# Weights on 128 partitions, and a first image load split over two queues, in a 3x3 convolution

## The chip, the cores and the metric

The kernel runs on one core of a Trainium2 chip. The metric is the time of one execution on the device in microseconds, the median of several. The core has a matrix engine (TensorE, PE in the profile, with PEld for its weight loads), a vector engine (VectorE, DVE), a scalar engine (ScalarE, ACT), a general one (GpSimd, POOL) and SyncE (SP), which in this kernel only issues DMAs. The 16 DMA engines are shared by all queues: SP's queue is q1 in the profile, ScalarE's is q10. Matmuls write PSUM; everything else lies in SBUF.

## The reference

A 3x3 convolution with padding 1 over 16 images of 64 channels and 64x64 pixels, float32, with 64 output channels, and a residual of the output's shape added:

```
x: (16, 64, 64, 64)   weight: (64, 64, 3, 3)   residual: (16, 64, 64, 64)
output[b, co] += weight[co, ci, kh, kw] * x_pad[b, ci, kh:kh+h, kw:kw+w]   # for all b, co, ci, kh, kw
return output + residual
```

The images, the residual and the output are 16.8 MB each.

## The kernel before, in words

**Data.** Two images make a pair: 128 partitions (image and channel) by 4096 pixels, one DMA of 2 MB with a row of 16 KB for each partition. There are 8 pairs. Three buffers `xr` hold pairs of images as they come; eight buffers `ro`, one for each pair, hold the residual, to which the result is added in place, and which is then stored. ScalarE casts each image to bf16 into one of four buffers `xp`, even rows of pixels into partitions 64 to 127 (line 159) and odd rows into partitions 0 to 63 (line 163), so that one matmul with 128 rows works on two rows of pixels at once.

**Weights.** ScalarE's queue loads them (line 151) as 64 partitions (output channel) by 576 numbers (input channel and tap). TensorE transposes the nine taps with an identity matrix that GpSimd makes (line 195), into PSUM buffer 0. VectorE casts six blocks of 64x192 from there into `wl` (line 172), in the layout of the stationary operand: d is which of two neighbouring rows, kw the column of the tap, and par says whether the output row is even or odd. GpSimd zeroes the two blocks that no tap fills (lines 147 and 148). The last cast raises `s_bank` by 2, which lets TensorE use both PSUM buffers.

**The convolution.** For each image, TensorE runs six steps (kw, d) of four matmuls each: four chunks of 8 row pairs by 64 columns, a whole PSUM buffer in all (line 83 issues a matmul with its weight load, line 84 one without). That makes 24 matmuls an image, 384 in all. Two PSUM buffers take turns. It waits for `s_bank` (the buffer is free) and `s_pack` (the image is cast) before each image. VectorE adds the residual in two instructions for each image (line 182) and raises `s_add`.

**Order of the work.** All waits are written out by hand.
- SP's program: pair 0 of the images (line 71), put by `to_the_front` ahead of everything else in its program, then residual 0, images 1, residual 1 and so on. From the fourth pair on, an image load waits on `s_half` until ScalarE has done with the buffer. The stores of pairs 0 to 4 (line 77) follow, each behind a wait on `s_add`. The stores of pairs 5 to 7 come after the critical section, which ends when all engines are done with it.
- ScalarE's program: the weights' DMA, then for each image its two casts; the first image of a pair waits for the landing of that pair (`s_x`).
- TensorE's program: a wait for the identity and the zeroed parts (`s_id`), a wait for the weights (`s_w`), the nine transposes, then a loop over four rounds of four images.
- GpSimd's program: the identity, the zeroes of the padding rows, the zeroes in `wl`.

Of the kernel before, what the change touches and what calls it, by code (L numbers as in the profile page):

```python
# [8 lines left out]
FP32 = mybir.dt.float32  # L9
# [6 lines left out]
def kernel(  # L16
# [7 lines left out]
    nc = tc.nc  # L24
# [6 lines left out]
    NPIX = H * W  # L31
# [4 lines left out]
    NXR = 3  # L36
# [3 lines left out]
    res_bc = residual.rearrange("b c h w -> (b c) (h w)")  # L40
    out_bc = out.rearrange("b c h w -> (b c) (h w)")
    x_bc = x.rearrange("b c h w -> (b c) (h w)")
    w_flat = weight.rearrange("co ci kh kw -> co (ci kh kw)")

    pool = ctx.enter_context(tc.tile_pool(name="pool", bufs=1))
    psum = ctx.enter_context(tc.tile_pool(name="psum", bufs=1, space=bass.MemoryType.PSUM))

    ident = pool.tile([64, 64], FP32)
    ro = [pool.tile([128, NPIX], FP32, name=f"ro{p}") for p in range(NPAIR)]
    xr = [nc.alloc_sbuf_tensor(f"xr{i}", [128, NPIX], FP32) for i in range(NXR)]  # L50

    xp = [pool.tile([128, J + 1, W], BF16, name=f"xp{i}") for i in range(NXP)]
    wraw = nc.alloc_sbuf_tensor("wraw", [64, 576], FP32)
    wl = pool.tile([128, 2, 3, 2, 64], BF16)
    ps = [psum.tile([128, NCHUNK, JC, W], FP32, name=f"ps{i}") for i in range(2)]

    sem = lambda name: tc.alloc_semaphore(name)
    s_w = sem("s_w")
    s_x = [sem(f"s_x{i}") for i in range(NXR)]
    s_r = [sem(f"s_r{p}") for p in range(NPAIR)]  # L60
    s_out = sem("s_out")
    s_id = sem("s_id")
    s_wt = sem("s_wt")
    s_half = sem("s_half")
    s_pack = sem("s_pack")
    s_bank = sem("s_bank")
    s_conv = sem("s_conv")
    s_add = sem("s_add")

    def load_x(p):  # L70
        return nc.sync.dma_start(out=xr[p % NXR][:, :], in_=x_bc[128 * p : 128 * p + 128, :]).then_inc(s_x[p % NXR], 16)

    def load_ro(p):
        nc.sync.dma_start(out=ro[p][:, :], in_=res_bc[128 * p : 128 * p + 128, :]).then_inc(s_r[p], 16)

    def store(p):
        return nc.sync.dma_start(out=out_bc[128 * p : 128 * p + 128, :], in_=ro[p][:, :])

    def matmul(out_, lhsT, rhs, start, stop, ldweights):

        e = nc.tensor
        if ldweights:
            return e.matmul(out=out_, lhsT=lhsT, rhs=rhs, start=start, stop=stop, skip_group_check=True)  # L83
        return e.add_instruction(  # L84
            mybir.InstMatmult(
                name=nc.get_next_instruction_name(),
                engine=PE,
                ins=[e.lower_ap(rhs), e.lower_ap(lhsT)],
                outs=[e.lower_ap(out_)],
                start_tensor_calc=start,  # L90
                stop_tensor_calc=stop,
                tile_size=(128, 128),
                tile_position=(0, 0),
                bass_skip_group_check=True,
                ldweights=False,
            )
        )

    def to_the_front(dma):

        def fixed(ap):
            t = ap.bass_ap.tensor.name
            return mybir.PhysicalAccessPattern(
                ap=ap.ap, offset=ap.bass_ap.offset, dtype=ap.dtype, memref=t, memsetref=t + "_set", bass_ap=ap.bass_ap
            )

        front = nc.main_func.blocks[0].instructions
        here = nc.cur_bb.bb.instructions  # L110
        ins = here.pop()
        assert ins.name == dma.ins.name
        at = next(
            i for i, e in enumerate(front) if e.engine == mybir.EngineType.SP and isinstance(e, mybir.InstDrain)
        )
        front.insert(at, copy.replace(ins, ins=[fixed(a) for a in ins.ins], outs=[fixed(a) for a in ins.outs]))

    with tc.tile_critical(no_gpsimd_drain=True):  # L118

        for p in range(NPAIR):  # L120
            if p >= NXR:

                nc.sync.wait_ge(s_half, 2 * (p - NXR) + 3)
            i = load_x(p)
            if p == 0:
                to_the_front(i)
            load_ro(p)
        for p in range(NEARLY):
            nc.sync.wait_ge(s_add, 2 * p + 3)
            store(p).then_inc(s_out, 16)  # L130


        nc.gpsimd.memset(ident[:, :], 0.0).then_inc(s_id, 1)  # L133
        nc.gpsimd.wait_ge(s_id, 1)
        nc.gpsimd.affine_select(  # L135
            out=ident[:, :],
            in_=ident[:, :],
            compare_op=mybir.AluOpType.not_equal,
            fill=1.0,
            base=0,  # L140
            pattern=[[-1, 64]],
            channel_multiplier=1,
        ).then_inc(s_id, 1)
        for t in xp:
            nc.gpsimd.memset(t[0:64, 0, :], 0.0).then_inc(s_id, 1)  # L145
            nc.gpsimd.memset(t[64:128, J, :], 0.0).then_inc(s_id, 1)  # L146
        nc.gpsimd.memset(wl[0:64, 0, :, 1, :], 0.0).then_inc(s_id, 1)  # L147
        nc.gpsimd.memset(wl[64:128, 1, :, 0, :], 0.0).then_inc(s_id, 1)  # L148


        nc.scalar.dma_start(out=wraw[:, :], in_=w_flat[:, :]).then_inc(s_w, 16)
        for n in range(B):
            p, im = divmod(n, 2)
            hp = slice(64 * im, 64 * im + 64)
            x4 = xr[p % NXR].rearrange("q (j two w) -> q j two w", two=2, w=W)
            t = xp[n % NXP]
            if im == 0:
                nc.scalar.wait_ge(s_x[p % NXR], 16 * (p // NXR + 1))
            i = nc.scalar.copy(out=t[64:128, 0:J, :], in_=x4[hp, :, 0, :])  # L159
            i.then_inc(s_half, 1)  # L160
            if n >= NXP:
                i._wait_ge(s_conv, n - NXP + 1)
            nc.scalar.copy(out=t[0:64, 1 : J + 1, :], in_=x4[hp, :, 1, :]).then_inc(s_pack, 1)  # L163


        nc.vector.wait_ge(s_wt, 1)
        tpf = ps[0].rearrange("p c j w -> p (c j) w")

        blocks = ((0, 0, 0, 0), (1, 0, 0, 1), (1, 0, 1, 0), (0, 1, 0, 2), (0, 1, 1, 1), (1, 1, 1, 2))
        for half, d, par, kh in blocks:  # L170
            hp = slice(64 * half, 64 * half + 64)
            i = nc.vector.tensor_copy(out=wl[hp, d, :, par, :], in_=tpf[0:64, 3 * kh : 3 * kh + 3, :])  # L172
        i.then_inc(s_bank, 2)
        for n in range(B):
            p, im = divmod(n, 2)
            hp = slice(64 * im, 64 * im + 64)
            o4 = ro[p].rearrange("q (j two w) -> q j two w", two=2, w=W)
            psj = ps[n % 2].rearrange("q c j w -> q (c j) w")
            if im == 0:
                nc.vector.wait_ge(s_r[p], 16)  # L180
            for par in range(2):
                i = nc.vector.tensor_tensor(  # L182
                    out=o4[hp, :, par, :], in0=psj[64 * par : 64 * par + 64, :, :], in1=o4[hp, :, par, :], op=ADD
                )
                if par == 0:
                    i._wait_ge(s_conv, n + 1)

                i.then_inc(s_add if par == 0 or n == B - 1 else s_bank, 1)


        nc.tensor.wait_ge(s_id, 4 + 2 * NXP)
        nc.tensor.wait_ge(s_w, 16)
        wraw3 = wraw.rearrange("p (ci t) -> p ci t", t=9)
        for t in range(9):
            i = nc.tensor.transpose(out=ps[0][0:64, t // 8, t % 8, :], in_=wraw3[:, :, t], identity=ident[:, :])  # L195
        i.then_inc(s_wt, 1)
        with nc.Fori(0, B // NXP, 1, engines=[PE]):
            for n in range(NXP):
                nc.tensor.wait_ge(s_bank, 1).then_inc(s_bank, -1)
                nc.tensor.wait_ge(s_pack, 1).then_inc(s_pack, -1)  # L200
                order = [(1, 0), (1, 1), (0, 0), (0, 1), (2, 0), (2, 1)]
                for i, (kw, d) in enumerate(order):
                    xlo, xhi = max(0, 1 - kw), min(W, W + 1 - kw)
                    for c in range(NCHUNK):
                        j0 = JC * c
                        m = matmul(
                            ps[n % 2][:, c, :, xlo:xhi],
                            wl[:, d, kw, :, :].rearrange("q r c -> q (r c)"),
                            xp[n][:, j0 + d : j0 + d + JC, xlo + kw - 1 : xhi + kw - 1],
                            i == 0,  # L210
                            i == len(order) - 1,
                            c == 0,
                        )
                m.then_inc(s_conv, 1)
# [36 lines left out]
```

## Time and profile before

| | |
|---|---|
| median of 3 runs | 124.08 us (124.05 to 124.40) |
| the profiled execution's own time | 124.16 us |
| its span in the profile | 122.1 us |
| TensorE busy | 86.5 us, 71% |
| VectorE busy | 75.2 us, 62% |
| ScalarE busy | 62.0 us, 51% |
| GpSimd busy | 2.2 us |
| moved by DMA | 50.48 MB, mean 413 GB/s over the span |
| from issue to landing, median: images, residual, stores, weights | 17.6, 22.1, 28.7, 8.5 us |

The page of the profile gives the busy time of each engine, its busy share in 40 equal slices of the span (one digit each, in tenths), the DMA queues with packets, megabytes and the share of 16 engines' span, groups of instructions with their mean time and what ended the idle time before them, and the DMA issues. A row of a timeline is the start, the time from the first start to the last end of a run of like instructions, the engine, the line, what it writes from what, the number of instructions, and in brackets how long the engine was idle before and what released it. An engine's name with a q (SPq) is its sequencer, which issues DMAs. The 2.06 us between the span and the time of the profiled execution lie around the traced program.

### The profile page before, as it was taken

The page shows a single profiled execution, that of the slowest core. Times are in us where ns is not written, and L with a number is a line of the kernel's source. Part 1 is how long each engine was busy: PE and PEld are TensorE (multiplying, and loading weights), DVE is VectorE, ACT ScalarE, POOL GpSimd, SP SyncE. Part 2 cuts the span into 40 slices and gives each one's busy share as a digit, 9 for nine tenths or more (in the row PEclk, how much of TensorE's full clock was granted, in tenths as well). Part 3 has the DMA queues.
Part 4 walks back from the last instruction along what each step waited for, and adds up shares of the span by engine and source line. Part 5 has one row for each costly group of instructions (what it writes and reads, how often), then busy time and mean ns, then how long its engine had stood idle before and what let it go on. Part 6 is the DMA issues. An engine that isn't in the chain of part 4 may idle for free.

```text
span 122.1 us, 729 instructions
## 1 busy us (share of the span) xinstructions
PE 86.5 (71%) x389; PEld 10.4 (9%) x105; DVE 75.2 (62%) x38; ACT 62.0 (51%) x33; POOL 2.2 (2%) x16
## 2 busy tenths in 40 slices
PE   0003799999999999999999999999999930000000
PEld 0003000101111010101010101111110100000000
DVE  0004101989889898898989889898798988000000
ACT  4009948966984993992994896699000000000000
POOL 5100000000000000000000000000000000000000
PEclk9999999999999999999999999999999999555555
DMA  6999999999999999999999999999999999999993
GB/s 182 408 348 429 429 429 429 429 424 429 429 429 424 429 429 429 429 429 429 429 429 419 429 429 424 429 429 429 435 435 435 429 429 429 435 435 429 429 429 140
DMA packets 3536, 50.48 MB, mean 413 GB/s; under 512 B 400, under 2 KB 400, under 8 KB 464
## 3 DMA queue, kind: packets, MB, share of 16 engines
q1 hardware_dynamic: 3456, 50.33, 97.8%
q10 hardware_dynamic: 80, 0.15, 0.4%
HBM read 33.70 MB, written 16.78 MB: 413 GB/s over the span
## 4 chain that ended last, share of the span: by engine, by line
PE 70%; DVEq 2%; DVE 2%; issue 0%
PE ps L84 53%; PE ps L83 17%; DVEq L118 2%; DVE ro L182 2%
## 5 line engine op out<-in xcount | busy, mean ns | idle before, releaser
L182 DVE TENSOR_TENSOR ro<-ps,ro 64x2048 f32<-64x2048 f32 x32 | 73.2, 2289 | 17.4 <-PE ps L84 16.9
L84 PE MATMUL ps<-xp,wl 128*128 128x504 bf16 (+1 forms) x288 | 79.9, 387 | 0.2
L159 ACT CAST xp<-xr 64x2048 bf16<-64x2048 f32 x16 | 30.3, 1896 | 21.3 <-DMA xr<-in_x_dram 21.1
L83 PE MATMUL ps<-xp,wl 128*128 128x504 bf16 (+1 forms) x92 | 35.6, 387 | 2.4 <-PEq L200 2.4
L163 ACT CAST xp<-xr 64x2048 bf16<-64x2048 f32 x16 | 30.4, 1897 | 0.4
L83 PEld LDWEIGHTS ps<-xp,wl 128*128 128x128 bf16 x96 | 9.5, 99 | 77.5 <-issue 77.5
L172 DVE CAST wl<-ps 64x192 bf16<-64x192 f32 x6 | 1.9, 347 | 10.9 <-PE ps L195 10.8
L195 PE MATMUL ps<-ident,wraw 64*64 64x64 f32 x9 | 1.1, 305 | 9.6 <-DMA wraw<-in_weight_dram 9.6
L159 ACT ACT_TABLE_LOAD x1 | 1.3, 1283 | 1.5 <-SPq L118 1.5
L195 PEld LDWEIGHTS ps<-ident,wraw 64*64 64x64 f32 x9 | 0.9, 163 | 9.6 <-issue 9.6
L146 POOL MEMSET xp<- 64x64 bf16 x4 | 0.6, 147 | 0.2
L145 POOL MEMSET xp<- 64x64 bf16 x4 | 0.6, 145 | 0.2
L148 POOL MEMSET wl<- 64x192 bf16 x1 | 0.3, 253 | 0.1
L147 POOL MEMSET wl<- 64x192 bf16 x1 | 0.3, 252 | 0.1
L135 POOL TENSOR_SCALAR_AFFINE_SELECT ident<-ident 64x64 f32<-64x64 f32 x1 | 0.2, 233 | 0.2 <-POOL ident L133 0.2
L133 POOL MEMSET ident<- 64x64 f32 x1 | 0.1, 145 | 0.5 <-SPq L118 0.5
L235 POOL MEMSET const-bfloat16-1.0<- 128x1 bf16 x1 | 0.1, 113 | 0.0
L235 POOL MEMSET const-uint8-127<- 128x1 uint8 x1 | 0.1, 112 | 0.0
L235 POOL MEMSET const-float32-1.0<- 128x1 f32 x1 | 0.1, 109 | 0.0
L235 POOL MEMSET const-float32-0.0<- 128x1 f32 x1 | 0.1, 104 | 0.2 <-issue 0.2
## 6 DMA issues: line engine op xcount, KB each, us to landing
xr<-in_x_dram SPq DMA_DIRECT2D x8, 2048.0 KB, 17.6
ro<-in_residual_dram SPq DMA_DIRECT2D x8, 2048.0 KB, 22.1
out_dram<-ro SPq DMA_DIRECT2D x8, 2048.0 KB, 28.7
wraw<-in_weight_dram ACTq DMA_DIRECT2D x1, 144.0 KB, 8.5
```

Of the source, the lines that this page charges most:

```text
L83: return e.matmul(out=out_, lhsT=lhsT, rhs=rhs, start=start, stop=stop, skip_group_check=True)
L84: return e.add_instruction(mybir.InstMatmult(name=nc.get_next_instruction_name(), engine=PE, ins=[e.lower_ap(rhs), e.lower_ap(lhsT)], outs ...
L118: with tc.tile_critical(no_gpsimd_drain=True):
L145: nc.gpsimd.memset(t[0:64, 0, :], 0.0).then_inc(s_id, 1)
L146: nc.gpsimd.memset(t[64:128, J, :], 0.0).then_inc(s_id, 1)
L147: nc.gpsimd.memset(wl[0:64, 0, :, 1, :], 0.0).then_inc(s_id, 1)
L159: i = nc.scalar.copy(out=t[64:128, 0:J, :], in_=x4[hp, :, 0, :])
L163: nc.scalar.copy(out=t[0:64, 1 : J + 1, :], in_=x4[hp, :, 1, :]).then_inc(s_pack, 1)
L172: i = nc.vector.tensor_copy(out=wl[hp, d, :, par, :], in_=tpf[0:64, 3 * kh : 3 * kh + 3, :])
L182: i = nc.vector.tensor_tensor(out=o4[hp, :, par, :], in0=psj[64 * par : 64 * par + 64, :, :], in1=o4[hp, :, par, :], op=ADD)
L195: i = nc.tensor.transpose(out=ps[0][0:64, t // 8, t % 8, :], in_=wraw3[:, :, t], identity=ident[:, :])
L235: nc = _bacc.Bacc("TRN2", target_bir_lowering=False, num_devices=1)
```

## The change

- The weights are loaded as 128 partitions of 288 numbers: half a row (32 input channels) of each output channel on each partition.
- The identity is 128x128. Each of the nine transposes takes 128 partitions by 32 channels and writes 32 partitions by 128 columns of PSUM.
- A block of `wl` is now filled by two casts of 32x192, one for each half of the input channels, which read PSUM with a step of two columns. There are 12 casts: VectorE does those of four blocks, ScalarE those of the other two, after the casts of image 0. Both raise `s_wt`, and TensorE waits for 3 on it (one for its own transposes, one for each of the two engines) before the loop. `s_bank` is raised at VectorE's first cast.
- The first image load is split by columns: pixels 0 to 2047 of pair 0 go by SP's queue, pixels 2048 to 4095 by ScalarE's queue, each at the front of its engine's program; the weights' DMA follows the second half in ScalarE's queue. Waits on `s_x` of buffer 0 count one DMA more.
- GpSimd waits for the identity before it goes on to the zeroes.

```diff
-    w_flat = weight.rearrange("co ci kh kw -> co (ci kh kw)")
+    w_rows = weight.rearrange("co (h ci) kh kw -> (co h) (ci kh kw)", h=2)
...
-    ident = pool.tile([64, 64], FP32)
+    ident = pool.tile([128, 128], FP32)
...
-    wraw = nc.alloc_sbuf_tensor("wraw", [64, 576], FP32)
+    wraw = nc.alloc_sbuf_tensor("wraw", [128, 288], FP32)
...
-    def load_x(p):
-        return nc.sync.dma_start(out=xr[p % NXR][:, :], in_=x_bc[128 * p : 128 * p + 128, :]).then_inc(s_x[p % NXR], 16)
+    def load_x(p, engine=nc.sync, cols=slice(0, NPIX)):
+        return engine.dma_start(out=xr[p % NXR][:, cols], in_=x_bc[128 * p : 128 * p + 128, cols]).then_inc(
+            s_x[p % NXR], 16
+        )
...
         at = next(
-            i for i, e in enumerate(front) if e.engine == mybir.EngineType.SP and isinstance(e, mybir.InstDrain)
+            i for i, e in enumerate(front) if e.engine == ins.engine and isinstance(e, mybir.InstDrain)
         )
...
+    blocks = ((0, 0, 0, 0), (1, 0, 0, 1), (1, 0, 1, 0), (0, 1, 1, 1), (0, 1, 0, 2), (1, 1, 1, 2))
+    tp = ps[0].rearrange("p c j w -> p c (j w)")
+
+    def weight_block(h, half, d, par, kh):
+
+        at = 64 * half + 32 * h
+        return dict(out=wl[at : at + 32, d, :, par, :], in_=tp[0:32, kh, 0:384].rearrange("p (kw co h) -> p kw co h", kw=3, h=2)[:, :, :, h])
...
-            i = load_x(p)
             if p == 0:
-                to_the_front(i)
+                to_the_front(load_x(p, cols=slice(0, NPIX // 2)))
+            else:
+                load_x(p)
             load_ro(p)
...
-            pattern=[[-1, 64]],
+            pattern=[[-1, 128]],
             channel_multiplier=1,
         ).then_inc(s_id, 1)
+        nc.gpsimd.wait_ge(s_id, 2)
...
-        nc.scalar.dma_start(out=wraw[:, :], in_=w_flat[:, :]).then_inc(s_w, 16)
+        to_the_front(load_x(0, nc.scalar, slice(NPIX // 2, NPIX)))
+        nc.scalar.dma_start(out=wraw[:, :], in_=w_rows[:, :]).then_inc(s_w, 16)
...
-                nc.scalar.wait_ge(s_x[p % NXR], 16 * (p // NXR + 1))
+                nc.scalar.wait_ge(s_x[p % NXR], 16 * (p // NXR + 1 + (p % NXR == 0)))
...
+            if n == 0:
+                nc.scalar.wait_ge(s_wt, 1)
+                for b in blocks[4:]:
+                    for h in range(2):
+                        i = nc.scalar.copy(**weight_block(h, *b))
+                i.then_inc(s_wt, 1)
...
         nc.vector.wait_ge(s_wt, 1)
-        tpf = ps[0].rearrange("p c j w -> p (c j) w")
-
-        blocks = ((0, 0, 0, 0), (1, 0, 0, 1), (1, 0, 1, 0), (0, 1, 0, 2), (0, 1, 1, 1), (1, 1, 1, 2))
-        for half, d, par, kh in blocks:
-            hp = slice(64 * half, 64 * half + 64)
-            i = nc.vector.tensor_copy(out=wl[hp, d, :, par, :], in_=tpf[0:64, 3 * kh : 3 * kh + 3, :])
-        i.then_inc(s_bank, 2)
+        for k, b in enumerate(blocks[:4]):
+            for h in range(2):
+                i = nc.vector.tensor_copy(**weight_block(h, *b))
+                if k == h == 0:
+                    i.then_inc(s_bank, 2)
+        i.then_inc(s_wt, 1)
...
         for t in range(9):
-            i = nc.tensor.transpose(out=ps[0][0:64, t // 8, t % 8, :], in_=wraw3[:, :, t], identity=ident[:, :])
+            i = nc.tensor.transpose(
+                out=tp[0:32, t // 3, 128 * (t % 3) : 128 * (t % 3) + 128], in_=wraw3[:, :, t], identity=ident[:, :]
+            )
         i.then_inc(s_wt, 1)
+        nc.tensor.wait_ge(s_wt, 3)
```

## The prediction

> **What bounds the kernel now.** I read the page's slices first, then its DMA queues.
>
> ```profile
> PE   0003799999999999999999999999999930000000
> ...
> DMA  6999999999999999999999999999999999999993
> ...
> q1 hardware_dynamic: 3456, 50.33, 97.8%
> q10 hardware_dynamic: 80, 0.15, 0.4%
> ```
>
> The 16 DMA engines are full from about 1 us until 120.8 us. SP's queue q1 alone takes 97.8% of them: 3072 packets of 16 KB, 192 an engine, at 0.611 us each in the packet records, are 117.3 us. That is the bound. But TensorE's work is almost as long, and it ends where the last stores are waiting for it. The timeline of the start, cut to the rows that carry the first convolution:
>
> ```profile
> 8.89 1.90 ACT L159 CAST xp<-xr 64x2048 bf16<-64x2048 f32 x1 [6.09 <-DMA xr<-in_x_dram]
> ...
> 9.63 1.14 PE L195 MATMUL ps<-ident,wraw 64*64 64x64 f32 x9 [9.63 <-DMA wraw<-in_weight_dram]
> 10.81 1.97 DVE L172 CAST wl<-ps 64x192 bf16<-64x192 f32 x6 [10.81 <-PE ps L195]
> 10.81 1.90 ACT L163 CAST xp<-xr 64x2048 bf16<-64x2048 f32 x1
> ...
> 13.12 0.58 PE L83 MATMUL ps<-xp,wl 128*128 128x512 bf16 x1 [2.35 <-PEq L200]
> ```
>
> Two arms meet at 13.1 us. Image: landing 8.87, two ScalarE casts, 12.71. Weights: landing 9.50, transposes, VectorE casts, 12.78. From there TensorE has no gap until 98.78 us (the groups of instructions have 2.4 us of idle time before line 83, all of it here, and 0.2 before line 84). And the timeline of the end:
>
> ```profile
> 98.78 4.61 DVE L182 TENSOR_TENSOR ro<-ps,ro 64x2048 f32<-64x2048 f32 x2 [0.58 <-PE ps L84]
> 103.68 1.76 SPq L77 DMA_DIRECT2D out_dram<-ro  x3
> ```
>
> The last three stores stand behind the end of the critical section, so they are issued at 103.68, after VectorE's last sum. The engines are then still writing the fifth store, whose landings spread from 105.64 to 106.57. So TensorE has little room: how little decides this case. At the start of the program an issue takes 1.01 (first engine) to 1.43 us (last one) to its first packet; for a store issued into an empty queue I take the same. With empty engines the end follows the issue by 1.43, a restart of 0 to 0.8 us (the 16 first packets of the run averaged 1.31 us for 0.61, the next ones 0.71; I take 0.3), and 24 packets, 14.75 us: 16.5 us. Before, the last packet ended 17.07 us after that issue (103.68 to 120.75). The room is thus 0.6 us (0.1 to 0.9), and every microsecond past it by which the convolution starts later is a microsecond at the end.
>
> **What the Trainium skill says.** "DMA: Bandwidth & Descriptors", section "Queues, rings and completion order": each DMA engine goes round between the queues that have work, a packet at a time. The trace agrees, with one addition. The DMA queues of two stretches, 0 to 5.2 us and 5.2 to 6.2 us:
>
> ```profile
> q1 hardware_dynamic: 86, 1.41, 79.0%
> ```
>
> ```profile
> q1 hardware_dynamic: 25, 0.41, 104.8%
> q10 hardware_dynamic: 25, 0.06, 14.6%
> ```
>
> 25 packets against 25: one 16 KB packet of q1 for each 2.3 KB packet of weights. The addition: the weights' DMA was issued at 0.95, and none of its packets ran before 5.2 us; on the engines that I followed by chaining starts to ends, five or six packets of q1 go first, the one under way and about four more that were already committed. The same page, "Issuing engines are not separate DMA queues": issuing from two engines saves only issue time; all runs on the same 16 DMA engines. So the split image moves no faster. "TensorE: Matmul & The Clock Gate", "Wait — 56ns, not 53.3ns?": from cold, start to start is N / 1.2 GHz. Here the first 128x512 matmuls start 0.427 apart, and the transposes with N=64 fp32 0.107. "VectorE: DVE Perf Modes", "Two Vector instructions with no wait between them": an instruction whose output starts in another quadrant of partitions is held until the one ahead is done. The six casts agree: starts 0.35 to 0.36 apart where the half changes, 0.27 where it stays.
>
> **The change part by part.** *Image split.* Same 2 MB on the same engines: 8 packets of 16 KB an engine become 8 of 8 KB on q1 and 8 on q10. Eight more packets cost below 0.1 us an engine; two queues may shorten the start, which lost 0.8 us an engine, so -0.5 to +0.2. It lies inside the DMA bound; I take 0. SP has as many issues as before, so none is late there; ACT's issue (its weights issue took 0.53) stands ahead of its drain (at 0.13 before) and may hold the opening barrier by 0.1 to 0.2 us, under the image's first 5 us of data.
>
> *Weights on 128 partitions.* Not 4 packets of 2.3 KB an engine but 8 of 1.15 KB; and in q10 they now stand behind the image's second half. While they go, q1 holds the first residual, in 16 KB packets. By the alternation, eight weight packets and the completion let some eight 16 KB packets go by, where four did. Estimate of the landing: 16 KB units x 0.615 + 2.0 (starts at 1.2, the ramp 0.8) + 1.5 or so from mean completion to the last engine's landing. The estimate gives 9.4 for before (9.5 units: eight of image, 0.6 of weights, one of residual; 5.9 + 3.5), measured 9.50. After, with:
> - both halves in step: 4 + 4 units of image, 8 of residual, 0.56 of weights: 16.6 units, 10.2 + 3.5 = 13.7
> - SP's half five packets ahead: q10 finishes four 16 KB packets later, 20.6 units, 12.6 + 3.5 = 16.1
> - ACT's half ahead by as much: 12.6 units, 7.7 + 3.5 = 11.2
>
> SP's first issue stands at 0.00, ACT's first instruction at 0.13, and ACT's issue takes longer; so SP's half is ahead, by three packets I say, between the first two: landing 15.0. That is 5.5 us later.
>
> *Transposes.* Still nine, but with 128 moving columns for 64. At N=64 they start 0.107 apart, so I take 0.213 (0.107 if loads of weights set the pitch): 8 x 0.213 + 0.41 = 2.1 for 1.14 us, +1.0 (0 to 1.0).
>
> *Casts.* The row has 347 ns for 64x192. Twelve half-blocks replace six; VectorE has eight of 32x192, each with another start quadrant than its neighbour: 7 x 0.357 + 0.35 = 2.85 for 1.97 us, +0.9. ScalarE's four: a 2048-wide cast takes 1.90, so 192 columns take some 0.35 by the same fixed part (the Trainium skill, "VectorE: DVE Perf Modes", "The TRN2 errata", prices a ScalarE copy out of PSUM at 172 cycles and one an element at 1.2 GHz, 0.30 us), 1.4 in all, beside VectorE's 2.85, hence nothing. ScalarE is free for them: image 0 lands by 11, its casts end by 15, and the transposes by 17.3. *The wait on s_wt for 3* comes ahead of the loop: 0 to 0.25, I take 0.1.
>
> What is queued behind these waits: on ScalarE, image 1's casts and then image 2's, whose first releases SP's fourth image load. Before, that load went at 20.63 while SP's queue held work until 33.4 (the landing of the third residual); at five to seven microseconds later it is still early, and so are the loads after it.
>
> *Larger identity, moved wait on POOL.* Its fills ended at 3.7 us; twice the columns add tenths. The weights land much later, which hides it; without that, tenths.
>
> *Sum.* Convolution from the weights' landing: 0.13 + 2.1 + 0.04 + 2.85 + 0.31 + 0.1 = 5.55 us, before 3.6. It starts at 15.0 + 5.55 = 20.5 for 13.1: 7.4 later. Less the 0.6 of room: +6.8 with these terms. The transposes and the start's cold stretch (12 matmuls at 0.427, it may be a few more or fewer at 0.21 each) can each give half a microsecond back, so I say +6.4. On the profiled execution: span 122.1 + 6.4 = 128.5 and the same 2.1 us around it, 130.6; the median of the runs, 124.08, stands 0.08 below the profiled execution's 124.16, so 130.5.
>
> **The rivals.** *ACT's half goes first.* Landing 11.2, convolution 16.75, 3.65 late: +3.05, 127.1. For it: nothing orders the two queues. Against it: SP's instruction starts first.
> *All of SP's half is committed ahead* (look-ahead counted in bytes, so eight packets of 8 KB): q10 starts behind it and alternates with 16 KB packets all along: about 24 units, landing 18.5, 11 late, some 134. For it: the four committed packets of before are 64 KB.
> *Not slower: weights pass by.* If the engines serve the short q10 packets together rather than one by one between residual packets, the weights land right behind the image. What decides is their landing: the longer chain costs 1.95 of itself, the room is 0.6, so only a landing before 8.2 us keeps the old end. Then the DMA bound stays, with up to 0.5 gained at the start: 123.5 to 124.4. For it: the queue that sets the bound isn't made longer. Against it: the 25 to 25 above; and the image's own data take until nearly 7.
> *The change doesn't do what it says*: the halves use the same engines, so nothing is doubled; that is in my sum already.
>
> **How the numbers follow.** SP's half ahead by none to five packets: 0.70, from 129 to 132.5, 130.5. ACT's ahead: 0.15. All of SP's half ahead, or a worse restart: 0.08. Not slower: 0.07, of it 0.03 for a gain of over 0.3%, which is about what this measurement can tell from no change. Slower 0.93, same 0.04, faster 0.03. Range 126.6 to 132.8: the first two cases nearly whole.
>
> **What would show it.** Right: weight packets of q10 between residual packets, landing at 13 to 16; transposes 0.21 apart, eight casts in 2.8; the first convolution at 19 to 22; a hole in the DMA slices near 106 to 112 us, ahead of the last three stores; the three issued at about 111. Wrong: the transposes start before 9.5, or the DMA row stays full to the end with a later convolution, which would mean that the room was larger than 0.6.

## The result, and the profile after

The changed kernel takes 129.01 us (median of six runs, 128.58 to 129.98) where the kernel before takes 124.18: a ratio of 1.0395, with a 95% interval of 1.0352 to 1.0437. It is slower, and by a little less than the 130.5 that was forecast. The profiled execution took 128.65 us, with a span of 126.8 for 122.1: +4.7 us.

The page of the kernel after, in the parts that answer to those shown of before:

```profile
PE   0000517999999999999999999999999990000000
...
DMA  6999999999999999999999999999999990199993
...
q1 hardware_dynamic: 3456, 49.28, 91.6%
q10 hardware_dynamic: 288, 1.20, 2.3%
```

The DMA row has a hole in slices 34 and 35 of the 40, where before it was full to the last slice. The convolution starts two slices later (the 5 ahead of it in TensorE's row is the transposes). The start, cut to the rows of the first convolution:

```profile
8.93 1.90 ACT L173 CAST xp<-xr 64x2048 bf16<-64x2048 f32 x1 [6.17 <-DMA xr<-in_x_dram]
10.85 1.90 ACT L177 CAST xp<-xr 64x2048 bf16<-64x2048 f32 x1
...
14.25 2.08 PE L214 MATMUL ps<-ident,wraw 128*32 128x128 f32 x9 [14.25 <-DMA wraw<-in_weight_dram]
16.37 1.27 ACT L182 CAST wl<-ps 32x192 bf16<-32x192 f32 x4 [3.62 <-PE ps L214]
16.45 2.89 DVE L189 CAST wl<-ps 32x192 bf16<-32x192 f32 x8 [16.45 <-PE ps L214]
...
19.77 0.58 PE L85 MATMUL ps<-xp,wl 128*128 128x512 bf16 x1 [3.44 <-PEq L222]
```

The image's arm is where it was: its casts run from 8.93 to 12.75, before from 8.89 to 12.71. Only the weights are late: they land at 14.12 us (before 9.50), and the chain behind them takes 5.65 us for 3.6. The convolution starts at 19.77, 6.64 us later. And the end:

```profile
104.91 4.61 DVE L201 TENSOR_TENSOR ro<-ps,ro 64x2048 f32<-64x2048 f32 x2 [0.58 <-PE ps L86]
109.81 1.78 SPq L79 DMA_DIRECT2D out_dram<-ro  x3
```

The last three stores are issued 6.13 us later than before. How DMA went meanwhile, from the table of stretches of the kernel after (start and end, length, busy time and instructions of PE, PEld, DVE, ACT and POOL, the granted clock of TensorE, the DMA engines' busy share, GB/s):

```profile
105.00:110.00 5.00, 0.00 (x0) 0.00 (x0) 4.49 (x2) 0.00 (x0) 0.00 (x0) 0.91 0.00 0
110.00:111.00 1.00, 0.00 (x0) 0.00 (x0) 0.00 (x0) 0.00 (x0) 0.00 (x0) 0.50 0.61 262
```

In five microseconds only VectorE works, and no byte moves. By the packet records the hole reaches from 105.40 to 110.64.

### The profile page after: what moved, and what is told of

It reads as the page before. It is cut to its first block, busy times and chain, and to the rows that moved or that the text cites. A ratio compares the mean times of both kernels' runs of the same rounds, so it can differ in the third digit from the quotient of the medians.

```text
span 126.8 us, 741 instructions
## 1 busy us (share of the span) xinstructions
PE 87.2 (69%) x393; PEld 10.7 (8%) x105; DVE 76.0 (60%) x40; ACT 63.2 (50%) x37; POOL 2.4 (2%) x16
## 4 chain that ended last, share of the span: by engine, by line
PE 67%; DVEq 2%; DVE 2%; issue 0%
PE ps L86 50%; PE ps L85 17%; DVEq L129 2%; DVE ro L201 2%
## 5 line engine op out<-in xcount | busy, mean ns | idle before, releaser
L189 DVE CAST wl<-ps 32x192 bf16<-32x192 f32 x8 | 2.8, 348 | 16.6 <-PE ps L214 16.4
L214 PE MATMUL ps<-ident,wraw 128*32 128x128 f32 x9 | 2.1, 416 | 14.3 <-DMA wraw<-in_weight_dram 14.3
L182 ACT CAST wl<-ps 32x192 bf16<-32x192 f32 x4 | 1.2, 308 | 3.7 <-PE ps L214 3.6
L214 PEld LDWEIGHTS ps<-ident,wraw 128*32 128x32 f32 x9 | 1.2, 141 | 14.7 <-issue 14.2
```

The costliest lines, as they stand in the source:

```text
L182: i = nc.scalar.copy(**weight_block(h, *b))
L189: i = nc.vector.tensor_copy(**weight_block(h, *b))
L214: i = nc.tensor.transpose(out=tp[0:32, t // 3, 128 * (t % 3) : 128 * (t % 3) + 128], in_=wraw3[:, :, t], identity=ident[:, :])
```

## The experiments

All comparisons are with runs of the kernel before on the same chip, whose medians were 124.15 to 124.21. "Landing" is that of the weights, "start" the first matmul of the convolution.

| kernel | landing | start | last three stores issued | median us | ratio to before, 95% interval |
|---|---|---|---|---|---|
| before | 9.50 | 13.13 | 103.68 | 124.18 | |
| changed | 14.12 | 19.77 | 109.81 | 129.01 | 1.0395 (1.0352 to 1.0437) |
| split only | 12.83 | 16.47 | 107.24 | 125.91 | 1.0122 (1.0095 to 1.0150) |
| 128 partitions only | 10.85 | 16.51 | 107.34 | 125.69 | 1.0101 (1.0051 to 1.0150) |

**Each half of the change alone.** First the image split without the new weights:

```diff
 # before, with the changed kernel's load_x, to_the_front and count on s_x
-                to_the_front(i)
+                to_the_front(load_x(p, cols=slice(0, NPIX // 2)))
...
+        to_the_front(load_x(0, nc.scalar, slice(NPIX // 2, NPIX)))
         nc.scalar.dma_start(out=wraw[:, :], in_=w_flat[:, :]).then_inc(s_w, 16)
```

> The kernel before with only the image split: pixels 0 to 2047 by SP's queue, 2048 to 4095 by ScalarE's queue, both at the front; the weights stay on 64 partitions (4 packets of 2.3 KB an engine) and follow the image half in ScalarE's queue. Theory (each weight packet waits for one packet of the other queue): four packets fewer than in the changed kernel, 4 x 0.62 us, so the weights land at 11.6 instead of 14.1; the chain behind them is the old 3.6 us, the convolution starts at 15.2; by the rule that the span is the convolution's start plus 107.3 (changed kernel: 126.8 - 19.8 + 0.3 for its shorter cold stretch), 122.5, some 124.5 us in all. Rival (the cut into 128 partitions makes the delay, the place in the queue does not): the weights land near 9.5 as before, 123.3 to 124.1 us.

Then the new weights with the old image load:

```diff
 # the changed kernel
-                to_the_front(load_x(p, cols=slice(0, NPIX // 2)))
+                to_the_front(i)
...
-        to_the_front(load_x(0, nc.scalar, slice(NPIX // 2, NPIX)))
         nc.scalar.dma_start(out=wraw[:, :], in_=w_rows[:, :]).then_inc(s_w, 16)
```

> The changed kernel with the image load of before: the whole first pair by SP's queue, nothing of it in ScalarE's. The weights on 128 partitions, the 128-wide transposes and the twelve casts stay. Theory: eight weight packets wait for eight of SP's where four did, so they land at 9.5 + 4 x 0.62 = 12.0; 5.6 us of chain, the convolution starts at 17.6, span 124.9, some 126.9 us. Rival (the image half ahead of the weights makes the whole delay): landing near 9.5, convolution at 15.1, 124.4 us.

Neither rival holds, and both landings were missed, in opposite directions: 12.83 for the expected 11.6, 10.85 for the expected 12.0. So were the times, 125.91 for 124.5 and 125.69 for 126.9. The sums had one price for both kinds of weights, and the packet records show two. From the first weights packet to the last it took 3.05 us in before and 3.14 with the split only, where each engine has four of them, and 4.89 us in both kernels with eight: 1.8 us more, where four packets at 0.62 would make 2.5. The last landing then followed the last packet by 1.17 to 1.24 us with 64 partitions and by 0.94 with 128. The part on the stream's lead, below, has the slower packets behind the first of these. The delays of the convolution add up all the same: 3.34 us for the split, where the landing makes all of it, and 3.38 for the 128 partitions, where the landing makes 1.35 and the longer chain 2.0. The sum is 6.72, and the whole change has 6.64. The times do not add up: +1.7 and +1.5 against +4.8, because the end hides 1.6 to 1.9 us of either delay, by the medians, and hides it once.

**Do the two queues take turns by packets, or by bytes?** In the kernel after, the DMA queues from 8.3 to 13.2 us, while the weights' packets run (queue: packets, MB, share of 16 engines):

```profile
q1 hardware_dynamic: 132, 1.90, 90.6%
q10 hardware_dynamic: 132, 0.15, 8.3%
```

132 against 132, although the one kind has 16 KB and the other 1.15. The test makes SP's packets smaller and leaves their bytes:

```diff
     def load_ro(p):
-        nc.sync.dma_start(out=ro[p][:, :], in_=res_bc[128 * p : 128 * p + 128, :]).then_inc(s_r[p], 16)
+        parts = 4 if p == 0 else 1
+        for c in range(parts):
+            cols = slice(c * NPIX // parts, (c + 1) * NPIX // parts)
+            nc.sync.dma_start(out=ro[p][:, cols], in_=res_bc[128 * p : 128 * p + 128, cols]).then_inc(s_r[p], 16)
...
-                nc.vector.wait_ge(s_r[p], 16)
+                nc.vector.wait_ge(s_r[p], 64 if p == 0 else 16)
```

> The changed kernel with the first residual loaded in four DMAs of a quarter of its columns, so packets of 4 KB instead of 16 KB; same bytes, same order in SP's queue. Theory (one packet against one, whatever their size): some 13 packets of ScalarE's queue (image and weights) wait 0.15 instead of 0.61 us each, the weights land about 5.5 us earlier, near 8.6; the convolution starts near 14.2, and the end is set by DMA again, 123.3 to 123.8 us. Rival (the queues share by bytes or by time): the weights land near 14 as in the changed kernel, 128.6 to 129.4 us.

The weights land at 10.01, 4.1 us earlier than in the changed kernel, and the time falls to 124.68 (ratio to before 1.0039, 1.0020 to 1.0058). From 7.2 to 9.5 us, while the weights run:

```profile
q1 hardware_dynamic: 158, 0.58, 76.2%
q10 hardware_dynamic: 153, 0.16, 21.1%
```

Again one packet against one. Sharing by bytes or by time is ruled out. The gain is short of the expected 5.5 us, and the end is therefore not quite set by DMA: a hole of 1.5 us is left ahead of the last stores. The 4 KB packets took 0.20 us each in this stretch, not the 0.15 that was assumed, and with 0.06 for a packet of weights a turn took 0.25 us. That is part of the miss; the rest is open.

**How much room has the end?** Twelve more casts on VectorE delay the convolution and touch no DMA:

```diff
 # before
+    spare = nc.alloc_sbuf_tensor("spare", [128, 12, 192], BF16)
...
+        for b, (half, d, par, kh) in enumerate(2 * blocks):
+            nc.vector.tensor_copy(out=spare[64 * half : 64 * half + 64, b, :], in_=tpf[0:64, 3 * kh : 3 * kh + 3, :].rearrange("p a b -> p (a b)"))
         for half, d, par, kh in blocks:
```

> The kernel before with twelve more casts of the same kind on VectorE ahead of the six that fill wl, into a spare tile that nobody reads; all loads are unchanged. The convolution starts 12 x 0.328 = 3.9 us later, at 17.1. Theory with the room that the changed kernel's trace shows (start plus 107.3): span 124.4, some 126.4 us. The prediction's room of 0.6 us: 124.1 + 3.9 - 0.6 = 127.4 us. Rival (the start of the convolution is covered by DMA): 124.1 us.

The start moves by 3.81 us to 16.93, and the median is 126.52 (ratio 1.0175, 1.0135 to 1.0215): 2.3 us for 3.8. A late start alone, with the loads as they were, costs time at the end. For the size of the room the test decides less. The median lies by the 126.4 of the larger room, and the four runs, 126.00 to 126.98, stay below the 127.4 of the smaller. But in the profiled execution, which took 126.84, the last stores are issued 3.43 us later than before and the span is 2.93 longer: a room of 0.5. From that issue to the last packet it took 16.53 us here, and 15.63 to 15.74 in the changed kernel and in the three others above; the first packets of the 16 engines start over 0.61 us, in those four over 0.15. Why is open.

**Is the hole all?** The next edit leaves the late start and takes away what makes the last stores wait for VectorE's very last sum:

```diff
 # the changed kernel
-    NEARLY = 5
+    NEARLY = 8
```

> The changed kernel with all eight stores inside the critical section (NEARLY 8 instead of 5), each behind its own wait on s_add, so that the stores of pairs 5 and 6 no longer stand behind VectorE's very last sum. Nothing at the start is changed. Theory (the time is lost only in the hole ahead of the last three stores): the hole closes or nearly so, only the last store needs the last sum, near 109.6, and then it has 4.9 us to go; DMA sets the end, and its stream is 0.9 us ahead of before's: span 121.3 to 122, 123.3 to 124 us, although the convolution starts as late as in the changed kernel. Rival (something else in the late start costs time): it stays near 128 to 129 us.

123.24 us, 0.9925 of before (0.9910 to 0.9940). The convolution starts at 19.51, VectorE ends at 109.44, as late as in the changed kernel, and the hole is gone. The page and the stretch that held the hole:

```profile
DMA  6999999999999999999999999999999999999992
```

```profile
104.00:110.00 6.00, 0.80 (x4) 0.00 (x0) 4.83 (x3) 0.00 (x0) 0.00 (x0) 0.93 0.99 423
```

So the whole loss lies in the hole. The control gives the edit to the kernel before:

```diff
 # before
-    NEARLY = 5
+    NEARLY = 8
```

> The kernel before with all eight stores inside the critical section, and nothing else: the control for the changed kernel with that edit. Theory (before is bound by its DMA stream, and has 1.4 us of room at the end): no change, 124.0 to 124.3 us. Rival (the place of the last stores costs time of itself): 123.3 us, as the changed kernel with this edit.

124.55, which is 1.0026 of before (1.0013 to 1.0040): no gain, rather a loss of 0.3 us, which neither the theory nor the rival had. The traces show where most of it lies: from the last packet to the end of the span it is 1.66 us, before 1.34, and all three versions with early stores have 1.66 or 1.67. So this edit makes the program's end 0.3 us longer. The early stores are no gain of themselves; they remove what the late start costs.

**Where does the stream's lead come from?** With the stores early, the changed kernel is 0.9 us faster than before. Not all of this is the stream: the span of the profiled execution is 0.65 us shorter, and the rest lies outside the span. The time of a run exceeds its span by 2.06 to 2.10 us, on average, in before and in three of the variants, and by 1.76 to 1.82 in all with the new weights. The version with the twelve casts, which has the old weights, also has 1.81, so the weights are not the reason, and it stays open. But the DMA stream is ahead: in the changed kernel the second pair of images has landed at 17.80, before at 18.69; at 18.34 with the split only, and at 17.83 with the 128 partitions only. Most of the lead comes with the new weights. Beside weights that go to 64 partitions, the 16 KB packets take 0.75 us on average in before (0.92 at most); beside weights on 128 they take 0.611, like nearly all others. To see whether the alternation of two queues matters, the old weights were put into SP's own queue:

```diff
 # before
             if p == 0:
                 to_the_front(i)
+            if p == 0:
+                nc.sync.dma_start(out=wraw[:, :], in_=w_flat[:, :]).then_inc(s_w, 16)
             load_ro(p)
...
-        nc.scalar.dma_start(out=wraw[:, :], in_=w_flat[:, :]).then_inc(s_w, 16)
```

> The kernel before with the weights' DMA moved to SP's queue, right behind the first pair of images; 64 partitions as before. No packets of two queues alternate. The 16 KB packets beside the weights took 0.65 to 0.87 us in before, 0.611 in the changed kernel. Theory A (the slow packets come from weights on 64 partitions, in whichever queue): the stream stays where it was, 124.0 to 124.3 us. Theory B (they come from the alternation of two queues): the stream is 0.5 us or more ahead, 123.4 to 123.7 us. In both the weights land near 8 and the convolution starts by 12.8.

124.26, ratio 1.0008 (0.9996 to 1.0020): theory A. The convolution starts at 12.84, as expected, but the weights land at 9.21 and not near 8: on 64 partitions the move to SP's queue brings them only 0.3 us forward. The next edit is the same with the new weights, and only the split left out:

```diff
 # weights on 128 partitions, whole image on SP's queue
             if p == 0:
                 to_the_front(i)
+            if p == 0:
+                nc.sync.dma_start(out=wraw[:, :], in_=w_rows[:, :]).then_inc(s_w, 16)
             load_ro(p)
...
-        nc.scalar.dma_start(out=wraw[:, :], in_=w_rows[:, :]).then_inc(s_w, 16)
```

> The weights on 128 partitions with transposes and casts as in the changed kernel, the image whole on SP's queue, and the weights' DMA in SP's queue right behind it. If the late landing behind other packets is what costs the time, and the stream's 0.9 us of lead comes from the weights' 128 partitions: weights land at 7.5 to 8, convolution 5.65 us later, near 13.5, DMA sets the end, span 121.2, 123.3 us, faster than before by 0.6 to 0.7%. Rival (the longer chain alone, 5.65 for 3.6 us, costs more than the room): 124.3 us or above.

123.20, ratio 0.9918 (0.9905 to 0.9932), faster than both kernels of the case. The stretch from 5.8 to 8.8 us of before, of the old weights on SP's queue, and of the new weights on SP's queue, one fence each; the last number is GB/s:

```profile
5.80:8.80 3.00, 0.00 (x0) 0.00 (x0) 0.00 (x0) 0.00 (x0) 0.00 (x0) 1.00 1.03 350
```

```profile
5.80:8.80 3.00, 0.00 (x0) 0.00 (x0) 0.00 (x0) 0.37 (x1) 0.00 (x0) 1.00 1.01 371
```

```profile
5.80:8.80 3.00, 0.56 (x3) 0.44 (x4) 0.00 (x0) 1.00 (x1) 0.00 (x0) 1.00 1.06 442
```

The engines are busy in all three; what they move differs. The view counts a packet whole where it starts. With packets shared out by their times, the three have 347, 377 and 425 GB/s, and the kernel with 128 partitions only has 428. So the old weights cost the stream 80 GB/s for three microseconds in ScalarE's queue, 0.56 us of its time, and 48 GB/s in SP's, 0.34 us. By the second pair of images the lead of the new weights is more, 0.86 and 0.90 us (17.83 for 18.69, 17.88 for 18.78); where it grows is open. So is whether the partitions do it or the packets, which are 2.3 KB in the old weights and 1.15 KB in the new: the two changed together in every run. The Trainium skill has a reason for the partitions, on "SBUF — State Buffer", section "Door 1: The DMA port swizzle": partitions 0 to 63 are reached through 8 of the 16 ports, and all 16 only by 128 partitions. That would fit, if the weights then crowd the 8 ports that half of the image rows need as well; but no run here shows a port, so this is argued and not shown.

The start of the fastest version:

```profile
8.24 2.08 PE L211 MATMUL ps<-ident,wraw 128*32 128x128 f32 x9 [8.24 <-DMA wraw<-in_weight_dram]
...
10.44 2.90 DVE L186 CAST wl<-ps 32x192 bf16<-32x192 f32 x8 [10.44 <-PE ps L211]
...
13.77 0.59 PE L83 MATMUL ps<-xp,wl 128*128 128x512 bf16 x1 [3.44 <-PEq L219]
```

The long chain is unchanged, but it begins at 8.1, and the convolution starts 0.6 us later than before. That is at the edge of the room: the last stores are issued at 104.39, their first packet runs at 105.23, and by the packet records only two or three of the 16 engines work from 104.8 to 105.2.

**Is the split to blame, then?** The changed kernel with the weights' DMA alone moved to SP's queue:

```diff
 # the changed kernel
             else:
                 load_x(p)
+            if p == 0:
+                nc.sync.dma_start(out=wraw[:, :], in_=w_rows[:, :]).then_inc(s_w, 16)
             load_ro(p)
...
-        nc.scalar.dma_start(out=wraw[:, :], in_=w_rows[:, :]).then_inc(s_w, 16)
```

> The changed kernel with one thing moved: the weights' DMA from ScalarE's queue, behind the image half, to SP's queue, behind the other half. Theory (queue position): the weights land at 7 to 8, ScalarE's half of the image near 8.5, its casts end by 12.4 and the weights' casts on ScalarE, which stand behind them, by 13.7, so the convolution starts near 14, just inside the room: 123.3 to 124.0 us. Rival (the split itself costs time): 125 us or more.

123.26, ratio 0.9927 (0.9913 to 0.9940), landing 8.06, start 13.72, and the DMA row of its page has no hole:

```profile
DMA  6999999999999999999999999999999999999992
```

One DMA issue in another queue is the difference between 129.0 and 123.3 us. The split does no harm where nothing waits behind it, and no good: 123.20 without it.

**The price of a cast.** VectorE's eight casts in an order in which neighbours share their 32 partitions:

```diff
 # weights on 128 partitions only
-        for k, b in enumerate(blocks[:4]):
-            for h in range(2):
-                i = nc.vector.tensor_copy(**weight_block(h, *b))
-                if k == h == 0:
-                    i.then_inc(s_bank, 2)
+        for k, (h, b) in enumerate((h, blocks[m]) for j in (0, 1) for h in range(2) for m in (j, 3 - j)):
+            i = nc.vector.tensor_copy(**weight_block(h, *b))
+            if k == 0:
+                i.then_inc(s_bank, 2)
```

> The kernel with the weights on 128 partitions and the whole image on SP's queue (weights in ScalarE's queue), with VectorE's eight casts put in another order, so that two neighbours write the same 32 partitions: pairs of 0, 32, 64, 96. Theory (a cast whose output starts in another quadrant waits for the one ahead): four of seven starts come 0.27 apart instead of 0.36, the casts take 2.55 instead of 2.89 us, the convolution starts 0.35 us earlier at the same landing, some 0.3 us less than 125.7. Rival (a cast of 32x192 has its price wherever it writes): 2.9 us.

The casts take 2.49 us for 2.89. Starts within a pair come 0.275 us apart, between pairs 0.35; in the old order all come 0.36 apart. The start moves from 16.51 to 16.10. The time, 125.55 for 125.69, is too noisy to tell. This bears out the rule of the Trainium skill on quadrants, groups of 32 partitions ("VectorE: DVE Perf Modes", "Two Vector instructions with no wait between them"), on which the prediction's price of the casts rested.

**Both remedies together.** The fastest version with its stores inside the critical section (`NEARLY` 8):

> The fastest so far (weights on 128 partitions, in SP's queue behind the whole first pair) with all eight stores inside the critical section. Theory: DMA sets the end already, so no change but for the tail's own spread, 123.1 to 123.3 us. Rival (its convolution, at 13.8, still holds the last stores back): 122.8 us.

123.34 (ratio 0.9935, 0.9918 to 0.9952): no gain in time. Within it two things cancel in the profiled executions: the last packet ends at 119.87 for 120.15, because the engines no longer wait for the last stores, and the program's end takes 1.67 us for 1.32. So the rival was right that the stores were held back a little, though not that the time would fall to 122.8.

## Why the prediction was right

Point by point, with the prediction's steps.

- *The queues take turns, a packet each; the weights stand behind the image half.* Right, and the smaller residual packets showed it. On the Trainium skill's page that the prediction names here, "DMA: Bandwidth & Descriptors", section "Queues, rings and completion order", a packet is typically some 9 to 17 descriptors; in these traces the turn is one packet of the profile, one row of a DMA, and the measurement decides. The forecast had SP's half three packets ahead, and so it was, as nearly as the records tell: 37 of SP's packets had started, 2.3 an engine, when the first engine turned to ScalarE's queue, and 53, 3.3 an engine, when the last one did. The landing was 14.12 for 15.0. What was off is the fixed part of the estimate, 3.5 us: it was fitted to the landing of before, and so held four packets at 0.75 us instead of 0.611 and 1.24 us from the last weights packet to the last landing. On 128 partitions these were 0.611 and 0.94, together 0.8 us less, which is nearly all of the miss. The part runs show the same term missed in both signs.
- *Image split: 0.* Right for the split (123.26 with it, 123.20 without). But the stream did gain, 0.9 us by the second pair of images, and the prediction had no term for what the old weights cost the packets beside them. In the changed kernel the gain bought nothing: the last packet ahead of the hole ended at 105.40, and that of the same store in before at 105.97, so the stream ran dry 0.6 us earlier and the hole became longer.
- *Transposes and casts.* 2.08 us for the 2.1 forecast and 2.89 for 2.85. The transposes start 0.213 us apart, which is twice the N / 1.2 GHz that the prediction quotes, as were the 0.107 of before; it took its price from the trace, and so came out right. ScalarE's four casts took 1.27, inside VectorE's. The chain was 5.65 for 5.55, the convolution's start 19.77 for 20.5.
- *The room at the end: 0.6.* The mis-sized term. The last stores came 6.13 us later (6.64 of start, less 0.51, since nine starts at the slow spacing were seen where before had twelve), and the span grew by 4.73. So the room was 1.4. The issue took 0.83 us to its first packet, on all engines within 0.15 us, not up to 1.43, and the stores had no slow first packets: 24 packets in 14.8 us. From issue to last packet this is 15.63 for 16.5. Of the six profiled executions with such a hole, five had 15.63 to 15.74 and a room of 1.3 to 1.4; the one with the twelve casts had 16.53 and 0.5. The forecast's value occurs, but it is the exception.
- *The sum.* 6.64 - 0.51 - 1.40 = 4.73, for the 6.4 forecast. Two sizes erred the same way, 0.9 us of landing and 0.8 of room.
- *The rivals.* ScalarE's half first, all of SP's half ahead, and weights that pass by did not occur. The last rival's deciding point, a landing before 8.2 us, was met by the two versions with the new weights on SP's queue: they land at 8.1, and no loss is left.

## What to carry to other kernels

A DMA that is small but urgent should not stand in a queue beside a stream of large packets: each of its packets waits for one of theirs, so cutting it into twice as many packets doubles the number that it waits for (3.1 us from first to last became 4.9). In the stream's own queue the new weights landed 2.7 us sooner with the whole image ahead of them, 6.1 us sooner with the split one; the old ones, with half as many packets, only 0.3. A kernel that DMA fills to 98% can still be bound by its compute engines at the end, if the last stores wait for the last result: find out how much later they could be issued, and charge that room once for all delays together. What the part runs cost alone does not say what they cost together.

## What was not expected of the hardware

- A 147 KB load onto 64 partitions, in packets of 2.3 KB, slowed the 2 MB loads beside it: 16 KB packets at 0.75 us on average instead of 0.611, and 0.3 to 0.6 us of the stream's time within three microseconds. The same bytes on 128 partitions, in packets of 1.15 KB, cost nothing beyond their own time, although they are twice as many packets, of 51 ns each.
- After a hole of 1.5 to 5.2 us, stores restart without a slow first packet: 0.61 to 0.62 us on average for the first 16 in all six executions, and 24 packets an engine in 14.8 to 14.9 us in five of them (15.7 in the one with the twelve casts). The loads at the start of the program had first packets of 1.31 us on average in before.
- Where the convolution sets the end, the times scatter more: 128.58 to 129.98 for the changed kernel, but 123.22 to 123.28 with its stores early. The number of slow matmul starts at the beginning differed between the profiled executions, from 8 to 14 at some 0.2 us each. This would make such a scatter. It was not tested, but the record speaks for it. The profile gives the granted clock of TensorE as half at the end (0.50 in the stretch from 110 us above) and counts it as full before that; by the mean clock of each run, the three fastest runs of the changed kernel spent 17.8 to 18.0 us at half clock, the three slowest 16.7 to 17.3. A later restart of the stores would make that time longer; it is shorter.
